# A hybrid decoder layer on one core: seven products for w_down in twelve steps of the second group, and weight loads kept in program order

## The chip, the cores and the metric

The kernel runs on one core of a Trainium2 chip. The metric is the device time of one execution in microseconds (us). Times of several runs are given as a median; a profile is one execution of its own, with its own time.

## The reference, cut to what matters

The reference is one inference step of a layer with two head groups (an mLSTM and a sliding-window attention), an output projection, and an MLP with a squared ReLU, for a prompt of 2048 tokens and a small decode batch of 32 rows. All arithmetic is in float32. The part around the change is

```python
mix = jnp.concatenate([y_m, y_a], axis=-1) @ lp['w_out']
x = x + rms_norm(mix, lp['norm_mix_post'])
u = rms_norm(x, lp['norm_ffn_pre'])
f = jnp.square(jax.nn.relu(u @ lp['w_up'])) @ lp['w_down']
x = x + rms_norm(f, lp['norm_ffn_post'])
x = x + jax.nn.sigmoid(x @ lp['w_pgate']) * (p @ lp['w_pproj'])
```

with D = 1024 model columns, 4096 hidden columns (w_up is 1024 x 4096, w_down 4096 x 1024), and 16 blocks of 128 tokens.

## The kernel before, in words

**Matmuls in three passes.** Every operand is split into a high part h (a cast on ScalarE, ACT) and a low part l (the value less h, on VectorE or on GpSimd, POOL), and `mm3` adds three matmuls, hh + hl + lh, into PSUM. A weight tile of 128 x 512 thus needs a transfer, a cast and a subtraction the first time. Weights that are used again are stored as a pair of parts in DRAM (`keep`, `store`; tensors wk), and later uses load the pair (512 KB) with no arithmetic.

**The ring of weights.** `Ring` hands out weights in the order of `plan()`. It has five raw tiles (wr, 256 KB, L296) and seven tiles for pairs (w). `take(n)` (L338) makes the next n. `row` (L348) is one tile of 128 rows and 512 columns; `multi` takes two row blocks at once; `heads` puts one together from two transfers; `product` builds the seven combinations of a w_up block of 1024 x 256 from two transfers into tiles of the pool `wide` (wb). All loads go out on SyncE's queue (SP), as `dma`; POOL's queue, `put`, carries stores and some loads. Seven pair tiles allow the loads to run ahead of TensorE by some seven tiles.

**The order of the work.** The code is written out as one program, and instructions are put into each engine's order by the language's scheduler, which may move an instruction ahead of earlier ones if its operands and its tile are free sooner. An instruction given to `here` (L205) is kept behind the instruction that was written before it on the same engine. All matmuls go through `Flow.issue`, which does that, so TensorE's order is the program's. `Flow` also keeps a clock of its own, to which each matmul adds passes x columns / 2400 us (at least 0.107), and it has sides: generators that emit side work when the clock has passed the time that they asked for with `yield`. `tick()` steps a side whose time has come; `drain(s)` empties one, and `wait` moves the clock on while other sides are stepped. So the yields decide where in the program side work is written. The weight loads are not given to `here`.

**The stages.** First six chunks of tokens (three blocks each, the last two with two) go through the input projections, with attention (`swa`) and the mLSTM (`mls`) as sides. Then three groups follow, of two chunks each: (0 to 5), (6 to 11), and (12 to 15 with the decode rows). In each group: the output projection (`mix_mm`, tensors mo) of both chunks, the residual and norm (`mix_post`), the MLP (`mlp`, L1626), and the gate (`gate_mm`, pg). The gains of norms are broadcast into one tile by `gain` (L1451, a load on SP), from a pool with one buffer: gpost (for the output projection) and gffn (for the MLP's end) take turns in it, and `gffn = gain(...)` stands at the start of `mlp` (L1628).

**The MLP.** The 4096 hidden columns go in 16 steps of 256 (FS = 2 tiles of 128). Steps 0 and 1 (FAST) run one chunk after the other, and meanwhile VectorE builds sums of the normed input for the rest. From step 2 on both chunks go together: `up_both` (L1719) computes the four hidden tiles (two chunks, two tiles of 128 hidden columns) with seven products of half size in place of eight (a Strassen-Winograd form), each with 12 matmuls of 384 columns, 84 in all (tensors up). Then `down` (L1762) multiplies, for each chunk and each half of 512 output columns, the two hidden tiles with two rows of w_down: three blocks x 2 x 3 = 18 matmuls of 512 columns (tensors dn), 72 in a step, and adds each PSUM result into the accumulator f with VectorE (L1759). In step 15 `finished` squares f for the norm and multiplies with gffn.

In the first group weights come raw and are split; in the second and third nearly all come as pairs from DRAM.

Of the kernel before, what the change touches and what calls it, by code (L numbers as in the profile page):

```python
# [9 lines left out]
F32 = mybir.dt.float32  # L10
# [8 lines left out]
P = 128  # L19
# [51 lines left out]
LODVE = 2  # L71
STEPS = FF // (FS * P)
STORE = 2
EMBW = 3.0
# [124 lines left out]
def hybrid_layer(ctx: ExitStack, tc: tile.TileContext, A, O):  # L199
    nc = tc.nc  # L200
    act, dve, pool = nc.scalar, nc.vector, nc.gpsimd
    pe = Flow(tc)
    swa, mls, tsp = pe.side(), pe.side(), pe.side()
    dma, put = nc.sync.dma_start, nc.gpsimd.dma_start
# [48 lines left out]
    def wsplit(hi, lo, src, eng=None):  # L253
        act.copy(hi, src)  # L254
        ins = (eng or weng()).tensor_tensor(lo, src, hi.bitcast(F32), ALU.subtract)  # L255
        if pinned:
            here(ins)

    class Ring:

# [23 lines left out]
        def get(self, key, n, make):  # L284

            t = self.tile(n)
            self.store()
            if key in self.kept:
                dma(t.bitcast(U32), self.kept[key])
# [9 lines left out]
        def product(self, key, i, src):  # L299


            def make(h, l):
                if i == 0:
                    self.blocks = []
                    for e in range(2):
                        t = self.wide.tile([P, KT // 2, 2 * P], F32, tag="w", name=f"{self.nm}b{self.n}{e}")
                        dma(t, src[e * 512 : (e + 1) * 512].rearrange("(k p) n -> p k n", p=P))
                        self.blocks += [t[:, :, :P], t[:, :, P:]]
# [39 lines left out]
        def row(self, key, src, n):  # L348
            def make(h, l):
                raw = self.load(n)  # L350
                dma(raw, src)
                wsplit(h, l, raw)

            return self.get(key, n, make)

        def heads(self, key, src, j, n):


            def make(h, l):
                raw = self.load(n)  # L360
                for s in range(2):
                    o = s * 256 + j * AD
                    dma(raw[s * AD : (s + 1) * AD], src[o : o + AD])
                wsplit(h, l, raw)

            return self.get(key, n, make)

        def multi(self, key, srcs, kn, n):
            three = lambda v: v.rearrange("p (k n) -> p k n", k=kn)

            def make(h, l):
                raw = self.load(kn * n)
                for off, w, s in srcs:
                    dma(three(raw)[:, :, off : off + w], s)
                wsplit(h, l, raw)
# [3 lines left out]
        def pairs(self, key, segs):  # L379


            def make(h, l):
                raw = self.load(512)
                for s, src in enumerate(segs):
                    dma(raw.rearrange("p (k s n) -> p k s n", k=2, s=2)[:, :, s], src)
                v = raw.rearrange("p (k s j c) -> p k j s c", k=2, s=2, j=2)
# [12 lines left out]
    def plan():  # L399
# [32 lines left out]
        def two(s, q):  # L432
            rows = w_up[q * P : (q + 2) * P, s * FS * P : (s + 1) * FS * P].rearrange("(k p) n -> p k n", p=P)
            return ("u", s, q), lambda key: ring.multi(key, [(0, FS * P, rows)], 2, FS * P)

        def rows_down(s):
            for half in range(2):
# [3 lines left out]
        for gi in range(len(GROUPS)):  # L441
# [12 lines left out]
            for s in range(FAST, STEPS):  # L454
                for i in range(7):
                    yield product(s, i)
                yield from rows_down(s)
            for ci in range(2):
                for half in range(2):
                    embed = 0 if half == 0 and ci == 0 else 4  # L460
                    for k in range(KT):
# [3 lines left out]
                        yield row(w_pg, k, half)  # L465

    ring.set_plan(plan())
    tpA = ctx.enter_context(tc.tile_pool(name="tpA", bufs=1))
    jp = ctx.enter_context(tc.tile_pool(name="jp", bufs=1))
# [1151 lines left out]
    wp = es2.enter_context(tc.tile_pool(name="wp", bufs=WBUF, reuse_waits="tile"))  # L1621
    sp2 = es2.enter_context(tc.tile_pool(name="sp2", bufs=2, reuse_waits="tile"))
    open_lp()
    dec = pe.side()

    def mlp(gi, chunks, sample):  # L1626
        nonlocal gffn
        gffn = gain(A["norm_ffn_post"], f"gffn{gi}")  # L1628
        G = f"{gi}"
        if sample:  # L1630
            f["t"] = es2.enter_context(tc.tile_pool(name="ft", bufs=1, reuse_waits="tile")).tile(
# [19 lines left out]
        def hidden(s, ci, ft, t, src, hid):  # L1651
# [6 lines left out]
            if sample:  # L1658

                for e, y in enumerate(hid[ci, ft]):  # L1660
# [3 lines left out]
                    else:  # L1664
                        pool.tensor_copy(y[:, W : W + HS], hid["s", ft, e])

        def temp(nm, n):
# [51 lines left out]
        def up_both(s, X, hid):  # L1719

            W = X[0][0].shape[2]
            nm = f"{G}{s}"
            turn = iter(X)

            def product(n):
                ps = psum(ps_s, f"up{nm}{n}")[:, :W]
                w, x = ring.take()[0], next(turn)
                for k in range(4):
                    mm3(ps, [t[:, k] for t in w], [t[:, k] for t in x], k == 0, k == 3)
                    pe.tick()  # L1730
                return ps

            t = [wp.tile([P, UW], F32, tag="re", name=f"re{nm}{n}")[:, :W] for n in range(4)]
# [52 lines left out]
        for ci in range(2):  # L1786
            if ci == 1:
# [4 lines left out]
                tp = es_t.enter_context(tc.tile_pool(name="tp", bufs=1, side="right", reuse_waits="tile"))  # L1792
                ring.wide = es_t.enter_context(tc.tile_pool(name="wide", bufs=WIDE, side="right", reuse_waits="tile"))
                tsp.add(sums())
# [8 lines left out]
        last_sum()  # L1803
        for s in range(FAST, STEPS):
            hid = {}
            up_both(s, X, hid)
            if s == STEPS - 1:
                es_t.close()
                open_lp()
# [195 lines left out]
```

## Time and profile before

| | us |
|---|---|
| median of 3 runs | 2610.94 (2605.71 to 2612.57) |
| the profiled execution, its time | 2623.78 |
| its span, first to last instruction | 2621.7 |
| TensorE busy in 1575.53 to 1951.77 (steps 2 to 13, second group) | 376.24 of 376.24 |
| TensorE busy in 100 to 680 (chunks 1 to 5) | 555.9 of 580 |
| TensorE busy in 780 to 1290 (first group's MLP) | 502.03 of 510 |
| TensorE busy in 2200 to 2530 (third group's MLP) | 330.00 of 330 |

Lines of the profile name engines PE (TensorE's matmuls), PEld (its weight loads), DVE (VectorE), ACT, POOL and SP; SPq is SP's queue, in which the transfers of weights wait their turn. L148 is the line of every matmul, so matmuls are told apart by their tensors' names. A row of the timeline has the start, the time, the engine, line, operation, output and inputs, the number of instructions merged, and in brackets how long the engine stood before and who released it. A row of groups has the count, the busy time, the mean of one in ns, and the idle time before. A row of waits has the time in total, how often, and the longest. Matmuls overlap, so the time of one is read from the distance between starts. PEclk is the clock that TensorE was granted, 1.00 being all of it.

### The profile page before, as it was taken

Reading aid. Unit: us, or ns where it says so; the run is one execution under the profiler, and the core shown is the slowest. Engines: PE = TensorE matmul, PEld = TensorE weight load, DVE = VectorE, ACT = ScalarE, POOL = GpSimd, SP = SyncE. Lnnn points to the kernel's source line nnn. Section 1 sums busy time; section 2 is a strip of 40 time slices with the busy share of each in tenths; the row PEclk is TensorE's granted clock in tenths of the full one; section 3 lists DMA queues with packets and bytes.
Section 4 is the critical chain, followed back from the end, with each engine's and each line's share of the span. In section 5 each row is a group of like instructions: output and inputs, shape, how many; then the busy total and the mean of one; then the engine's idle time right before and its main releaser. Section 6 shows DMA issues by size and latency. Waiting matters only on the chain.

```text
span 2621.7 us, 39337 instructions
## 1 busy us (share of the span) xinstructions
PE 2534.7 (97%) x14260; PEld 2204.3 (84%) x14260; DVE 1483.0 (57%) x3162; ACT 974.3 (37%) x2167; POOL 620.3 (24%) x988
## 2 busy tenths in 40 slices
PE   7999999998999999999999999999999999999998
PEld 7787888777778888888877788999998879999986
DVE  6666656665657655656744654444446346444553
ACT  5545444544445444444523342222223134222231
POOL 5311111112433666666523200000001011000010
PEclk9999999999999999999999999999999999999999
DMA  9756656576898666666799765555556899777787
GB/s 315 273 192 201 207 181 213 194 244 227 260 343 287 254 250 253 244 254 251 271 341 318 255 201 188 188 191 188 187 187 233 295 334 359 253 255 256 256 299 235
DMA packets 220433, 651.10 MB, mean 248 GB/s; under 512 B 25397, under 2 KB 59401, under 8 KB 220224
## 3 DMA queue, kind: packets, MB, share of 16 engines
q1 hardware_dynamic: 170032, 474.02, 53.4%
q0 software_dynamic: 50160, 174.54, 17.3%
q8 instruction: 113, 1.85, 0.3%
q14 instruction: 80, 0.66, 0.1%
q10 hardware_dynamic: 48, 0.03, 0.0%
HBM read 494.34 MB, written 155.25 MB: 248 GB/s over the span
## 4 chain that ended last, share of the span: by engine, by line
PE 77%; DVE 8%; DMA 7%; issue 3%; ACT 2%; POOL 2%; SPq 0%; ACTq 0%; DVEq 0%; POOLq 0%
PE up L148 21%; PE dn L148 21%; PE mo L148 5%; PE pg L148 5%; PE v L148 3%; DMA w<-wk 3%; PE o L148 3%; DMA wk<-w 2%; PE qk L148 2%; PE qa L148 2%; PE gv L148 2%; DVE hl L232 2%; PE aT L152 1%; PE aO L148 1%; PE pv L148 1%
## 5 line engine op out<-in xcount | busy, mean ns | idle before, releaser
L148 PE MATMUL dn<-w,hh 128*128 128x512 f32 x1792 | 564.0, 396 | 6.3 <-ACT re L1654 3.8
L1759 DVE TENSOR_TENSOR f<-f,dn 128x512 f32<-128x512 f32 x420 | 286.9, 686 | 220.5 <-PE dn L148 218.4
L148 PEld LDWEIGHTS dn<-w,hh 128*128 128x128 f32 x1792 | 334.2, 189 | 84.7 <-DVE f L1759 6.8
L148 PE MATMUL dn<-w,hl 128*128 128x512 f32 x896 | 354.5, 396 | 1.6 <-DVE hl L232 1.6
L1734 DVE TENSOR_TENSOR re<-up,re 128x384 f32<-128x384 f32 (+1 forms) x294 | 151.9, 517 | 320.2 <-PE up L148 320.2
L148 PEld LDWEIGHTS dn<-w,hl 128*128 128x128 f32 x896 | 168.8, 188 | 43.5 <-DVE hl L232 5.1
L1735 ACT COPY re<-up 128x384 f32<-128x384 f32 (+1 forms) x42 | 18.8, 448 | 392.0 <-PE up L148 392.0
L1654 ACT ACTIVATE re<-re 128x384 f32<-128x384 f32 (+1 forms) x168 | 83.0, 494 | 207.5 <-DVE re L1734 203.9
L232 DVE TENSOR_TENSOR hl<-re,hh 128x384 fp32r<-128x384 f32 (+1 forms) x192 | 137.6, 717 | 16.8 <-ACT hh L231 15.7
L282 POOL DMA_DIRECT2D wk<-w x242 | 134.1, 556 | 34.4 <-DVE w L255 25.2
L254 ACT CAST w<-wr 128x512 fp32r<-128x512 f32 (+2 forms) x152 | 88.9, 597 | 95.9 <-PE up L148 32.3
L254 ACT CAST w<-wb 128x512 fp32r<-128x512 f32 x98 | 60.6, 620 | 168.4 <-PE dn L148 114.6
L255 POOL TENSOR_TENSOR w<-wr,w 128x512 fp32r<-128x512 f32 (+2 forms) x76 | 100.2, 1319 | 80.5 <-ACT w L254 79.5
L255 POOL TENSOR_TENSOR w<-wb,w 128x512 fp32r<-128x512 f32 x70 | 92.3, 1319 | 110.3 <-ACT w L254 109.8
L1460 POOL DMA_DIRECT2D x<-x1d x16 | 8.7, 545 | 463.5 <-PE up L148 449.4
L1655 ACT ACTIVATE re<-re 128x384 f32<-128x384 f32 (+1 forms) x192 | 94.9, 494 | 5.9
L231 ACT CAST hh<-re 128x384 fp32r<-128x384 f32 (+1 forms) x192 | 92.6, 482 | 8.3
L1067 ACT ACTIVATE s<-s,swt 128x257 f32<-128x257 f32 (+1 forms) x128 | 63.3, 496 | 65.8 <-DVE swt L1064 65.8
L1061 DVE CUSTOM_DVE_ANT_0 s<-aS,cst,sink 128x256 f32<-128x256 f32 (+1 forms) x128 | 57.1, 472 | 52.0 <-PE aS L148 51.6
L148 PE MATMUL up<-t2h,w 128*128 128x384 f32 (+1 forms) x336 | 85.1, 320 | 0.0
L148 PE MATMUL up<-t0h,w 128*128 128x384 f32 (+1 forms) x336 | 85.1, 320 | 0.0
L148 PE MATMUL up<-t1h,w 128*128 128x384 f32 (+1 forms) x336 | 85.1, 320 | 0.0
(1526 smaller groups left out, 6415.7 us busy)
## 6 DMA issues: line engine op xcount, KB each, us to landing
w<-wk SPq DMA_DIRECT2D x728, 512.0 KB, 4.9
wk<-w POOLq DMA_DIRECT2D x238, 512.0 KB, 7.2
wr<-in_w_down_dram SPq DMA_DIRECT2D x64, 256.0 KB, 8.2
wb<-in_w_up_dram SPq DMA_DIRECT2D x28, 512.0 KB, 6.9
w<-wk SPq DMA_DIRECT2D x20, 528.0 KB, 3.9
x<-in_x_prompt_dram SPq DMA_DIRECT2D x16, 512.0 KB, 4.4
y<-yd SPq DMA_DIRECT2D x32, 256.0 KB, 7.0
xr<-in_x_prompt_dram POOLq DMA_DIRECT2D x16, 512.0 KB, 9.4
```

Source lines behind the costliest of these rows:

```text
L148: ins = self.pe.matmul(out, lhsT, rhs, start=start, stop=stop)
L231: act.copy(hi, src)
L232: dve.tensor_tensor(lo, src, hi.bitcast(F32), ALU.subtract)
L254: act.copy(hi, src)
L255: ins = (eng or weng()).tensor_tensor(lo, src, hi.bitcast(F32), ALU.subtract)
L282: here(put(self.kept[key], t.bitcast(U32)))
L1061: dve.tensor_tensor_reduce(s_[:, s, lo : 2 * P], pS[:, s, lo:], bias[:, j, lo:], 1.0 if s == 0 else 0.0625, sink[:, h : h + 1], ALU.add, A ...
L1067: act.activation(e_, e_, AF.Exp, bias=nm[:, s : s + 1], accum_out=sm[:, s : s + 1])
L1654: act.activation(t, src, AF.Relu)
L1655: act.square(t, t)
L1734: add = lambda out, a, b: dve.tensor_tensor(out, a, b, ALU.add)
L1759: dve.tensor_tensor(out(i), out(i), ps, ALU.add)
```

## The change

There are two parts.

**Loads in the program's order.** Every weight load of the ring goes through `wload`, which gives it to `here`. Other loads on SP (gains, tokens, y, p, Wt) are as before.

**Seven products for w_down.** In the second group, for steps 2 to 13 taken in pairs, `up_seven` computes the four hidden tiles as `up_both` does and from them four block sums (s1 = a21 + a22, s2 = s1 - a11, s3 = a11 - a21, s4 = a12 - s2; a12 is chunk 0's second hidden tile), with splits. `down_seven` then does seven products, each over three blocks, both steps and three passes (18 matmuls), in place of eight: the hidden tiles and sums with three rows of w_down (k1 and k0 for the first half of columns, k1 for the second) and four differences of them. A product's PSUM result is added by VectorE into one or two places: parts of f, or a shared sum U of three tiles, two of which lie in the buffer of gpost and gffn. After step 13 `share` adds U into three quarters of f on POOL, and only then gffn is asked for in this group.

The differences are computed once: `differences`, a side (`prep`) added before chunk 1 of the projections, loads the four blocks of each step's w_down rows into four raw tiles, subtracts on VectorE, and stores four differences (td) to DRAM, all pinned. It is drained after the last chunk. In the second group they come as raw loads with a cast on ACT and a subtraction on POOL. The pool `wide` is closed at step 2 of that group to make room, and `sp2` has one buffer for two.

```diff
+SEVEN = range(2, STEPS - 2)
+SGROUP = 1
+DIFW = 16.0, 4.0, 8.0
...
-    swa, mls, tsp = pe.side(), pe.side(), pe.side()
+    swa, mls, tsp, prep = [pe.side() for _ in range(4)]
...
+    def wload(out, src):
+
+        here(dma(out, src))
...
             if key in self.kept:
-                dma(t.bitcast(U32), self.kept[key])
+                wload(t.bitcast(U32), self.kept[key])
...
+        def diff(self, key, src):
+            def make(h, l):
+                raw = self.load(512)
+                wload(raw, src)
+                wsplit(h, l, raw, pool)
+
+            return self.get(key, 512, make)
...
+            for i, k, half in ((0, 1, 0), (0, 0, 0), (3, 0, 0), (4, 0, 0), (1, 0, 0), (0, 1, 1), (2, 0, 0)):
+                for s in steps:
+                    yield diff(s, i) if i else row(w_down, s * FS + k, half)
...
+    def differences():
+
+        sub = lambda out, a, b: here(dve.tensor_tensor(out, a, b, ALU.subtract))
+        for s in SEVEN:
+            b11, b21, b12, b22 = b = [ring.load(512) for _ in range(4)]
+            for n, t in enumerate(b):
+                k = s * FS + n % 2
+                here(put(t, w_down[k * P : (k + 1) * P, n // 2 * 512 : n // 2 * 512 + 512]))
+            yield DIFW[0]
+            for i, out, x, y in ((1, b11, b12, b11), (3, b12, b22, b12), (2, b22, b22, b11), (4, b21, b21, b22)):
+                sub(out, x, y)
+                yield DIFW[1]
+            for i, out in ((1, b11), (3, b12), (2, b22), (4, b21)):
+                here(put(td[s, i], out))
+            yield DIFW[2]
...
     for ci, blocks in enumerate(CHUNKS):
+        if ci == 1:
+            prep.add(differences())
         project(ci, blocks)
     pe.drain(swa)
+    pe.drain(prep)
...
     def mlp(gi, chunks, sample):
         nonlocal gffn
-        gffn = gain(A["norm_ffn_post"], f"gffn{gi}")
         G = f"{gi}"
+        if gi != SGROUP:
+            gffn = gain(A["norm_ffn_post"], f"gffn{gi}")
...
+            uses = (
+                ("12", out(0, 0)),
+                ("11", u, out(0, 0)),
+                ("s3", out(1, 1), out(1, 0)),
+                ("22", out(1, 0)),
+                ("s1", out(1, 1), out(0, 1)),
+                ("s4", out(0, 1)),
+                ("s2", u),
+            )
+            for n, (a, *to) in enumerate(uses):
+                w = [[t[:, :512] for t in w] for w in ring.take(2)]
+                for i in range(len(c0)):
+                    ps = psum(ps_mm, f"ds{G}{s}{n}{i}")
+                    for e in range(2):
+                        mm3(ps, [y[:, cols(i)] for y in As[e][a]], w[e], e == 0, e == 1)
+                        pe.tick()
+                    for m, o in enumerate(to):
+                        if first and n == 1 and m == 0:
+                            act.copy(o(i), ps)
+                        else:
+                            dve.tensor_tensor(o(i), o(i), ps, ALU.add)
+
+        def share(U):
+
+            for ci, half in ((0, 1), (1, 0), (1, 1)):
+                for i, b in enumerate(chunks[ci]):
+                    v = f[b][:, half * 512 : half * 512 + 512]
+                    pool.tensor_tensor(v, v, U[i], ALU.add)
...
         for s in range(FAST, STEPS):
+            if gi == SGROUP and s in SEVEN:
+                if s == SEVEN[0]:
+                    es_w.close()
...
+                    hq, wq = side("hq", 5), side("wq", 1)
+                    U = gp.tile([P, 2, 512], F32, tag="g", name=f"us{G}")
+                    U = [U[:, 0], U[:, 1], side("us", 1).tile([P, 512], F32, name=f"ut{G}")]
+                    As = []
+                As.append(up_seven(s, X, hq, wq))
+                if len(As) == 2:
+                    down_seven(s, As, U, s == SEVEN[1])
+                    As = []
+                if s == SEVEN[-1]:
+                    share(U)
+                    gffn = gain(A["norm_ffn_post"], f"gffn{gi}")
+                continue
             hid = {}
             up_both(s, X, hid)
```

More of the change, by code (lines that the diff above doesn't have):

```diff
@@ new lines, in share, with products, product @@
+        def share(U):
[3 more added lines that the diff above has]
+                    pool.tensor_tensor(v, v, U[i], ALU.add)
+        def products(s, X):
+            turn = iter(X)
+            def product(n):
+                ps = psum(ps_s, f"up{G}{s}{n}")[:, : X[0][0].shape[2]]
+                w, x = ring.take()[0], next(turn)
+                for k in range(4):
+                    mm3(ps, [t[:, k] for t in w], [t[:, k] for t in x], k == 0, k == 3)
+                    pe.tick()
+                return ps
+            return product
@@ L1722, in up_both @@
             nm = f"{G}{s}"
[L1723 to L1731, printed above, removed]
+            product = products(s, X)
             t = [wp.tile([P, UW], F32, tag="re", name=f"re{nm}{n}")[:, :W] for n in range(4)]
```

77 lines of the change are left out of this document (69 added, 8 removed).

## The prediction

> **What bounds the kernel now.** I read the page first, then the chain of work that ended last, then stages.
>
> ```profile
> span 2621.7 us, 39337 instructions
> ...
> PE 2534.7 (97%) x14260; PEld 2204.3 (84%) x14260; DVE 1483.0 (57%) x3162; ACT 974.3 (37%) x2167; POOL 620.3 (24%) x988
> ...
> PE 77%; DVE 8%; DMA 7%; issue 3%; ACT 2%; POOL 2%; SPq 0%; ACTq 0%; DVEq 0%; POOLq 0%
> ```
>
> TensorE is busy for 2534.7 of 2621.7 us, so only two things can move the time: fewer matmuls, or a change in the 87 us in which TensorE stands. The change does both. The chain shows the steps of the second group:
>
> ```profile
> 1575.53 14.74 PE up L148 x84
> 1590.27 16.80 PE dn L148 x72
> ...
> 1935.18 16.59 PE dn L148 x72
> 1951.77 14.70 PE up L148 x84
> ```
>
> Steps 2 to 13 are the twelve pieces of dn from 1590.27 to the end of the one at 1935.18; with their ups they fill 1575.53 to 1951.77, 376.24 us. The window table says how tight that is, beside two steps of the first group, which also split fresh weights:
>
> ```profile
> core 0: us, PE busy (x) PEld busy (x) DVE busy (x) ACT busy (x) POOL busy (x), PEclk, DMA share, GB/s
> 1575.53:1951.77 376.24, 376.24 (x1873) 338.60 (x1873) 170.04 (x279) 81.56 (x157) 0.00 (x0) 1.00 0.56 185
> 878.65:942.78 64.13, 63.65 (x314) 56.10 (x313) 38.43 (x54) 26.19 (x48) 40.33 (x45) 1.00 0.64 246
> ```
>
> TensorE has no gap there, the granted clock is 1.00, VectorE is at 45%, POOL does nothing. Matmuls taken out of this stage come off the end, if nothing else becomes late.
>
> **Part 1: seven products.** The 72 matmuls of one dn take 16.59 to 16.80 us, some 0.231 us each. Two steps need 144 now. Seven products, each over three blocks, two steps and three passes, are 126. Six pairs drop 6 x 18 = 108 matmuls, 108 x 0.231 = 24.9 us.
>
> What is added lies on other engines:
>
> ```profile
> L1759 DVE TENSOR_TENSOR f<-f,dn 128x512 f32<-128x512 f32 x420 | 286.9, 686 | 220.5 <-PE dn L148 218.4
> L1734 DVE TENSOR_TENSOR re<-up,re 128x384 f32<-128x384 f32 x196 | 108.8, 555 | 228.2 <-PE up L148 228.2
> L232 DVE TENSOR_TENSOR hl<-re,hh 128x384 fp32r<-128x384 f32 x128 | 109.3, 854 | 13.9 <-ACT hh L231 13.7
> L255 POOL TENSOR_TENSOR w<-wr,w 128x512 fp32r<-128x512 f32 x66 | 91.1, 1381 | 70.9 <-ACT w L254 70.0
> L254 ACT CAST w<-wr 128x512 fp32r<-128x512 f32 (+2 forms) x152 | 88.9, 597 | 95.9 <-PE up L148 32.3
> ```
>
> VectorE per pair: 30 accumulations for 24 (30 x 0.686 = 20.6 us), 16 adds of 384 columns (8.9) and 8 low parts (6.8): 36 us in 58.5 us of TensorE. Within the seven products it evacuates 20.6 us while TensorE takes 29.1; the tightest place is two products with two targets each, 12 x 0.686 = 8.2 us beside 8.3, behind three PSUM banks. ACT gains eight casts per pair, 4.8 us. POOL gets eight low parts of weights, 11.0 us, and twelve block sums or low parts of 384 columns, for which the trace has no row: between 1.04 us (1381 ns scaled by 384/512) and 1.38 us, so 12 to 17 us. Together 23 to 28 us in 58.5. All hidden on average. What is lost at the seams I bound from the first group: its two steps take 64.13 us where two of the second take 62.7, 1.4 us per pair with eleven split tiles a step against four here. I take 0.5 per pair, 3 us in all (0 to 9). Sum of part 1: -24.9 + 3 = -21.9 us.
>
> **Part 2: the differences of w_down.** Twelve times four subtractions (48 x 0.75 us, by the VectorE row of the same low part, below) and 96 transfers of 256 KB are put beside the projections of chunks 1 to 5.
>
> ```profile
> L255 DVE TENSOR_TENSOR w<-wr,w 128x512 fp32r<-128x512 f32 x66 | 49.3, 750 | 26.9 <-ACT w L254 24.5 <-PE ut31t L152 0.2
> 332.00:448.00 116.00, 113.50 (x758) 97.18 (x757) 75.64 (x239) 55.48 (x148) 14.18 (x36) 1.00 0.59 197
> 535.00:690.00 155.00, 144.71 (x995) 119.97 (x992) 91.23 (x280) 72.61 (x191) 37.92 (x73) 0.97 0.69 238
> ```
>
> VectorE is at 65% there and DMA at 59 to 69%; 36 us of VectorE and 25 MB over some 590 us raise these by about 6 and 12 points. TensorE's gaps are 2.5 us in a chunk of three blocks and 10.3 us over 535 to 690. I put 4 us on it, with the later start of the w_up blocks in the first group (0 to 14: the gaps doubled).
>
> The end of this work is another matter. Each step of the preparation asks for 16 + 4 x 4 + 8 = 40 us of the planner's clock. Summing that clock over its matmuls (passes x columns / 2400), chunks 1 to 5 last 488 us of it; twelve steps ask for 480, but each of 72 resumptions waits for the next tick, so eleven fit, and step 13 is left to the new drain. The drain runs the planner 41 us ahead, and whatever of the mLSTM's last chunk is due in those 41 us is written in front of the first w_out matmul, where now it lies between them:
>
> ```profile
> 681.35 0.66 PE L148 MATMUL mU<-vs,kw 128*64 128x130 f32 x8
> ...
> 700.72 0.66 PE L148 MATMUL mU<-vs,kw 128*64 128x130 f32 x8 [0.24 <-DVE num L1018]
> ```
>
> Six such pieces (about 4 us of TensorE), each waiting for VectorE, lose their cover: about 4 us. The preparation also holds four of the five raw tiles until its stores land, so w_out comes through one, some 6 us a tile, where two tiles last 4.2 us: another 4 us. Together 8 (2 to 18).
>
> **Part 3: loads in the program's order.** A load given to `here` is issued after whatever was written before it on SP, and SP waits in order:
>
> ```profile
> SPq L289 <- PE up L148: 331.5, 233, 11.2
> ...
> 725.22 0.38 SPq L374 DMA_DIRECT2D wr<-in_w_up_dram  x1
> 758.99 5.04 SPq L374 DMA_DIRECT2D wr<-in_w_up_dram  x3
> 773.16 0.33 SPq L1453 DMA_DIRECT2D gffn<-in_norm_ffn_post_dram  x1
> ...
> 2160.37 6.51 SPq L289 DMA_DIRECT2D w<-wk  x4
> 2169.60 0.33 SPq L1453 DMA_DIRECT2D gffn<-in_norm_ffn_post_dram  x1
> ...
> 772.46 0.68 DVE L1468 TENSOR_TENSOR f<-f,gpost 128x512 f32<-128x512 f32 x1
> ...
> 2168.88 0.69 DVE L1468 TENSOR_TENSOR f<-f,gpost 128x512 f32<-128x512 f32 x1
> ```
>
> In the code gffn (one buffer, shared with gpost) is asked for ahead of the first w_up load of each MLP. Today those loads pass it: they stand before it in SP's order. Pinned, they stand behind it, and gffn waits until VectorE has read gpost for the last time (the last two rows), after the end of mo. So the prefetch of seven weight tiles is gone at that seam. TensorE went on without a gap at these places:
>
> ```profile
> 769.25 0.35 PE L148 MATMUL up<-ut00h,w 128*128 128x384 f32 x1
> ...
> 2167.06 0.29 PE L148 MATMUL up<-ut20h,w 128*128 128x272 f32 x1
> ...
> 2176.73 0.39 PE L148 MATMUL up<-ut20h,w 128*128 128x272 f32 x1 [1.57 <-DMA w<-wk]
> ```
>
> The landing times by stage (w_down's raw tiles at 770 to 800, kept tiles at 2155 to 2200 and in steps 2 to 13), and what a long gap costs besides:
>
> ```profile
> DMA to landing us min/median/max: 3.9/6.5/8.0
> ...
> w<-wk SPq DMA_DIRECT2D x26, 512.0 KB, 6.0
> ...
> w<-wk SPq DMA_DIRECT2D x134, 512.0 KB, 4.3
> ...
> 790.00:800.00 10.00, 6.17 (x19) 4.54 (x18) 10.00 (x13) 6.37 (x14) 5.46 (x6) 0.69 0.97 361
> ...
> 795.52 1.22 PE L148 MATMUL dn<-w,hh 128*128 128x512 f32 x2 [3.83 <-ACT re L1654]
> ...
> 800.72 0.62 PE L148 MATMUL dn<-w,hh 128*128 128x512 f32 x2
> ```
>
> After 3.83 us of standing, the granted clock of the window is 0.69, and the twelve matmuls from 795.52 to 800.72 took 5.20 us where 12 x 0.231 = 2.8 are due: 2.4 us on top of the gap. The Trainium skill (TensorE: Matmul & The Clock Gate, What's actually happening) has the array at half clock after an idle window of about 3.4 us until a busy one of that length; an estimate by that page is 1.7 us a gap, which would make the sum 2 us smaller. The trace agrees in kind, and its 2.4 is used.
>
> First group: gffn at 773.16, the raw tile at 773.5, landed 6.5 later, cast 0.6, low part 0.75: 781.4, a gap of 12.1 from 769.25, with the slow clock 14.5. The gap at 795 (3.83 + 2.4) then finds VectorE and ACT ahead and goes: +8.3 (6 to 16). Third group: 2169.6 + 0.4 + 6.0 = 2176.0, 8.9 after 2167.06, with the clock 11.3, less the 1.57 gap there now: +9.7 (6 to 13).
>
> Second group: gffn moves behind the shared sums, whose tile has the same buffer. Let T be the end of the last product, whose three blocks take 1.39 us each and are summed 0.7 later. POOL's nine adds (1.38 us, by the low part's row above, the nearest) start at T - 2.1, wait for the third block's sum at T + 0.7, and have read that buffer for the last time, in the eighth, at T + 9.0. Only then gffn goes, and behind it the first w_up tile of step 14: 0.4 + 4.3 later, T + 13.7. Nothing else is left for TensorE. With the clock +16.1 (10 to 20).
>
> **Sum.** -21.9 + 4 + 8 + 8.3 + 9.7 + 16.1 = +24.2 us. The profiled execution has a span of 2621.7 and a time of 2623.78; the median of the runs is 2610.94, 12.8 below it. I expect a span near 2646 and a median of 2635.
>
> **Rivals.** (1) Faster, 2601: the three gains cost nothing, since SP is held less than I read; -21.9 + 12 = -9.9. It decides if the three gaps together stay under about 4 us. For it: the waiting of SP now is harmless for thousands of us, with tiles ahead. Against it: behind a gain no tile is ahead. The Trainium skill (DMA: Bandwidth & Descriptors, Anatomy of one DMA) says that a semaphore wait happens on the issuing sequencer before dispatch; by that rule this rival falls, and the SP rows above agree. Chance 0.12. (2) No change, 2618: half of the 34 us of gaps is covered, because VectorE frees gpost sooner when TensorE stands and POOL takes the adds whose sum is ready first: -21.9 + 12 + 17 = +7. Chance 0.14. (3) Slower by more, 2661: the preparation reaches TensorE. Step 13's loads, subtractions and stores run one after the other (loads 9.4 by the row below for POOL's queue, 3 of VectorE, 5 to store), the first raw tiles of w_out wait for them, and chunks 4 and 5 lose what DMA share they have: 30 us instead of 12 for part 2, and 8 more at the seams of the pairs: +24.2 + 18 + 8 = +50.
>
> ```profile
> xr<-in_x_prompt_dram POOLq DMA_DIRECT2D x16, 512.0 KB, 9.4
> ```
>
> For it: the gaps of 10.3 us there. Against it: 31% of DMA is free. Chance 0.14.
>
> **The numbers.** The forecast has 0.60 and a range of its own of 2619 to 2652. A measurement of this kernel can tell 0.3%, 7.8 us, from no change. Faster takes rival 1: 0.12. Within 0.3%: rival 2: 0.14. Slower: the forecast and rival 3, 0.74. The range reaches from rival 1, rounded down to 2600, to just past rival 3, 2664.
>
> **What would show it.** Right: in SP's queue each gffn directly ahead of the first w_up load of groups 1 and 3 and of step 14, TensorE idle there for 9 to 14 us waiting for a weight's transfer or its low part, and a granted clock under 1 just behind; six dn pieces of 126 matmuls and 29.1 us; POOL's nine adds ending some 9 us after the last product. Wrong: up starting directly behind mo or behind the last product; a product's 18 matmuls taking over 4.5 us; or a projection longer by over 15 us.

## The result, and the profile after

The changed kernel took 2678.03 us (median of 4 runs, 2673.33 to 2681.06) where the kernel before took 2610.86 (4 runs, 2605.71 to 2612.57): a ratio of 1.0259, with a 95% interval of 1.0239 to 1.0279. It is slower by 67 us, where the prediction had 24. The profiled execution took 2679.81 us with a span of 2678.0, 56 longer than the span before. Of all executions reported here one, of the kernel with four mends below, took 5642.95 us; it is left out, and its cause is open.

The head of the page after:

```profile
span 2678.0 us, 39855 instructions
...
PE 2527.9 (94%) x14152; PEld 2194.1 (82%) x14152; DVE 1538.8 (57%) x3255; ACT 1014.7 (38%) x2254; POOL 815.0 (30%) x1213
```

TensorE has exactly the 108 matmuls less (14260 to 14152), but is busy only 7 us less and stands for 150 us, not 87. The window table after (start and end; length; busy time and count of PE, PEld, DVE, ACT, POOL; clock, DMA share, GB/s) says where:

```profile
100.00:680.00 580.00, 554.07 (x3810) 471.05 (x3808) 389.86 (x1205) 271.42 (x725) 136.39 (x303) 0.99 0.72 253
680.00:780.00 100.00, 76.78 (x332) 59.62 (x333) 54.11 (x107) 37.54 (x83) 34.65 (x51) 0.86 0.80 273
...
1615.24:1991.54 376.30, 355.20 (x1765) 317.75 (x1763) 200.41 (x322) 123.42 (x243) 147.70 (x129) 0.99 0.60 198
```

The steps with seven products, up to the first up of step 14, take 376.30 us, as long as before (376.24), with 355.20 of TensorE in them. The w_out stretch (680 to 780) has a quarter of its time empty. TensorE's rows behind the longest gaps, and the first up of the third group, which has none:

```profile
685.69 1.53 PE L151 MATMUL mS<-qks,qks 64*128 64x128 f32 x8 [6.22 <-DVE m14f L990]
...
712.22 0.79 PE L151 MATMUL mo<-w,x6h 128*128 128x512 f32 x1 [7.53 <-ACT w L257]
...
796.45 0.69 PE L151 MATMUL up<-ut00h,w 128*128 128x384 f32 x1 [9.58 <-ACT w L257]
...
1599.53 0.72 PE L151 MATMUL dn<-w,hh 128*128 128x512 f32 x2 [4.22 <-ACT re L1703]
...
1991.54 0.69 PE L151 MATMUL up<-ut10h,w 128*128 128x384 f32 x1 [11.31 <-DMA w<-wk]
...
2210.15 0.29 PE L151 MATMUL up<-ut20h,w 128*128 128x272 f32 x1
...
2650.14 1.19 PE L151 MATMUL pg<-w,xt21h 128*128 128x512 f32 x2 [8.11 <-DMA w<-wk]
```

SP's own order at the first ups of the first group, of step 14 and of the third group, and in the last gate:

```profile
789.61 0.33 SPq L1501 DMA_DIRECT2D gffn<-in_norm_ffn_post_dram  x1
789.99 9.22 SPq L264 DMA_DIRECT2D wr<-in_w_up_dram  x7
...
1985.67 0.33 SPq L1501 DMA_DIRECT2D gffn<-in_norm_ffn_post_dram  x1
1986.11 12.49 SPq L264 DMA_DIRECT2D w<-wk  x9
...
2206.88 3.10 SPq L264 DMA_DIRECT2D w<-wk  x3
2212.68 0.33 SPq L1501 DMA_DIRECT2D gffn<-in_norm_ffn_post_dram  x1
...
2641.84 1.73 SPq L1994 DMA_DIRECT2D out_dram<-ot  x2
2645.90 0.33 SPq L1994 DMA_DIRECT2D out_dram<-ots  x1
2646.32 13.66 SPq L264 DMA_DIRECT2D w<-wk  x10
```

In the first group and ahead of step 14 the gain stands in front of the loads, as forecast. In the third group loads went in front of the gain and TensorE runs on. In the last gate the output stores of the first half (`finish` sends them through `dma` when `last` is set) stand in front of the weights of the second half and wait for the first half's last values. The prediction did not have that one.

To put a price on each stretch I follow the time at which TensorE starts a piece of work, after less before (us, from the timelines of the two profiled executions):

| start of | before | after | shift | added by the stretch that ends here |
|---|---|---|---|---|
| chunk 1 | 139.8 | 132.0 | -7.8 | chunk 0: -7.8 |
| chunk 5 | 575.5 | 576.3 | +0.8 | chunks 1 to 4: +8.6 |
| first w_out matmul | 680.6 | 695.2 | +14.7 | chunk 5 and the drain: +13.9 |
| w_out, second chunk | 726.9 | 749.0 | +22.1 | w_out, first chunk: +7.4 |
| first up, first group | 769.2 | 796.5 | +27.2 | the first gain: +5.1 |
| first gate | 1293.9 | 1318.6 | +24.8 | first MLP: -2.4 |
| w_out, second group | 1390.6 | 1422.0 | +31.3 | first gate: +6.5 |
| first up, second group | 1487.8 | 1517.1 | +29.3 | w_out, second group: -2.0 |
| step 2, second group | 1575.4 | 1615.1 | +39.7 | steps 0 and 1: +10.4 |
| step 14 | 1951.6 | 1991.5 | +39.9 | seven products and the gain behind them: +0.2 |
| first up, third group | 2167.1 | 2210.2 | +43.1 | steps 14 and 15, gate, w_out: +3.2 |
| last gate | 2535.1 | 2581.7 | +46.6 | third MLP: +3.5 |
| end of the span | 2621.7 | 2678.0 | +56.3 | last gate: +9.7 |

The two executions lie 12.8 and 1.8 us above the medians of their kernels, so the table adds up to 56.3 and not to 67. A row holds to some 3 us: in the run below in which only the last stores are moved, rows ahead of the last gate differ from these by up to 3.5 us, and by 11.4 in sum.

Within steps 2 to 13, the last product's matmuls end at 1980.2, 365.0 us after 1615.24. So twelve steps save 11.2 us in place of 21.9, and the gap of 11.31 takes that back. The chain of waits shows one seam, the same in all six pairs:

```profile
1615.24 23.19 PE up L151 x132
1640.23 5.60 DMA wr<-td
1645.84 1.57 POOL w L258 x2
1647.41 0.94 issue
1648.34 1.03 POOL s L1757
1649.96 0.60 DVE f L1796
1650.57 0.81 issue
1651.38 1.37 DVE hl13a L1727
1652.75 0.61 DVE f L1796
1653.40 22.59 PE ds L151 x96
```

A difference lands late; POOL waits to split it; the block sum s stands behind that on POOL; VectorE, which takes s3 out of the tile that POOL still reads, waits for s; and behind VectorE's wait stand the sums that free PSUM for TensorE.

### The profile page after: what moved, and what is told of

It reads as the page before. It is cut to its first block, busy times and chain, and to the rows that moved or that the text cites. A ratio compares the mean times of both kernels' runs of the same rounds, so it can differ in the third digit from the quotient of the medians.

```text
span 2678.0 us, 39855 instructions
## 1 busy us (share of the span) xinstructions
PE 2527.9 (94%) x14152; PEld 2194.1 (82%) x14152; DVE 1538.8 (57%) x3255; ACT 1014.7 (38%) x2254; POOL 815.0 (30%) x1213
## 3 DMA queue, kind: packets, MB, share of 16 engines
q0 software_dynamic: 57840, 199.71, 19.8%
## 5 line engine op out<-in xcount | busy, mean ns | idle before, releaser
L151 PE MATMUL dn<-w,hh 128*128 128x512 f32 x1216 | 383.4, 396 | 6.3 <-ACT re L1703 4.2
L151 PEld LDWEIGHTS dn<-w,hh 128*128 128x128 f32 x1216 | 226.1, 188 | 59.5 <-ACT re L1703 4.7
L1901 DVE TENSOR_TENSOR f<-f,dn 128x512 f32<-128x512 f32 x276 | 187.3, 686 | 138.9 <-PE dn L151 138.3
L151 PE MATMUL dn<-w,hl 128*128 128x512 f32 x608 | 240.1, 395 | 0.1
L258 POOL TENSOR_TENSOR w<-wr,w 128x512 fp32r<-128x512 f32 (+2 forms) x124 | 161.0, 1305 | 134.3 <-ACT w L257 110.8
L289 POOL DMA_DIRECT2D wk<-w x242 | 133.8, 555 | 17.3 <-DVE w L258 10.4
L1796 DVE TENSOR_TENSOR f<-f,ds 128x512 f32<-128x512 f32 x144 | 94.2, 683 | 30.1 <-PE ds L151 26.2
L258 DVE TENSOR_TENSOR w<-wr,w 128x512 fp32r<-128x512 f32 (+2 forms) x76 | 73.3, 970 | 53.0 <-ACT w L257 44.1
L1703 ACT ACTIVATE re<-re 128x384 f32<-128x384 f32 (+1 forms) x120 | 57.8, 482 | 112.3 <-DVE re L1876 108.9
L1738 DVE TENSOR_TENSOR re<-up,re 128x384 f32<-128x384 f32 x84 | 46.6, 555 | 83.2 <-PE up L151 83.2
L151 PE MATMUL up<-ut10h,w 128*128 128x384 f32 x288 | 80.6, 348 | 11.3 <-DMA w<-wk 11.3
L151 PE MATMUL up<-ut00h,w 128*128 128x384 f32 x288 | 80.1, 350 | 10.0 <-ACT w L257 9.6
```

Of the source, the lines that this page charges most:

```text
L151: ins = self.pe.matmul(out, lhsT, rhs, start=start, stop=stop)
L289: here(put(self.kept[key], t.bitcast(U32)))
L1703: act.activation(t, src, AF.Relu)
L1738: add = lambda out, a, b: dve.tensor_tensor(out, a, b, ALU.add)
L1796: dve.tensor_tensor(o(i), o(i), ps, ALU.add)
L1901: dve.tensor_tensor(out(i), out(i), ps, ALU.add)
```

## The experiments

Theory A: the loss has separate places, and most of them come from the loads' order: SP waits at a gain or a store with loads behind it, td loads come late, and the scheduler writes other engines' work in another order. The rest is the drain of the preparation. Theory B: the order has slack, and the seven products and their preparation cost what is lost. All ratios below are to the kernel before in the same session, whose median was 2610.15 to 2612.13. The changed kernel was timed in the first session alone, so what a mend gains on its 2678.03 us mixes sessions; the stretch in the profile in which the mend works is the surer number.

**Each part alone.** The kernel before with the ring's loads given to `wload`, and the changed kernel with

```diff
     def wload(out, src):
-        here(dma(out, src))
+        dma(out, src)
```

> The kernel before with one edit: the ring's weight loads are kept in program order (no seven products, no differences). Theory A (the order of the loads is the larger part of the loss): chunk 0 gains about 8 us; then TensorE stands about 9 us where the first group's w_up begins, about 9 us where the second group's begins (here its gain stands ahead of the loads again), not at the third group's (a pool is opened between), and about 8 us in the last gate behind the output stores; with the slow clock behind each gap 2635 to 2645 us against 2611. Theory B (the loss comes from the seven products and their preparation, the loads have slack): within 8 us of 2611.

Measured: 2651.94 us, ratio 1.0148 (1.0118 to 1.0177), 40 us slower, 7 more than theory A had at most. Its timeline has the gaps where theory A put them, and the third group has none; the one of 4.52 was not in the expectation:

```profile
769.42 0.69 PE L148 MATMUL up<-ut00h,w 128*128 128x384 f32 x1 [9.33 <-ACT w L254]
...
1500.30 0.66 PE L148 MATMUL up<-ut10h,w 128*128 128x384 f32 x1 [12.52 <-DMA w<-wk]
...
1582.45 1.22 PE L148 MATMUL dn<-w,hh 128*128 128x512 f32 x2 [4.52 <-ACT re L1658]
...
2628.02 1.19 PE L148 MATMUL pg<-w,xt21h 128*128 128x512 f32 x2 [8.11 <-DMA w<-wk]
```

> The changed kernel with the weight loads no longer kept in program order; seven products and differences stay. Theory A: the gaps of 9.6 us at 796, 11.3 at 1992 and 8.1 at 2650 go, and chunk 0 loses its 8 us again; the drain of about 17 us ahead of w_out and the pairs' 60.2 to 61.5 us stay: 2635 to 2650 us. Theory B: 2665 us or more.

Measured: 2623.26 us, ratio 1.0043 (1.0027 to 1.0058), better than theory A's numbers, which had the seams of the pairs stay. The drain is still there (first w_out matmul at 697.2), but steps 2 to 13 now take 354.20 us:

```profile
1595.90:1950.10 354.20, 353.60 (x1765) 318.53 (x1764) 201.69 (x324) 125.70 (x244) 139.82 (x122) 1.00 0.64 210
```

That is 22.0 less than the 376.24 before; part 1 of the prediction had 21.9. Seams and the gain's gap are both gone when the order alone is taken away. Theory B has fallen: the order alone costs 40 us, the other part alone 11. The remaining 16 of the 67 need both parts. By the profiles some 22 are in the seams' late td loads and the gain behind the shared sum, less one place that the change itself removes (the gain of the second group, a gap of 12.52 in the kernel with the order alone); the rest is not told apart.

**The gains.** `gffn` is asked for in step 15, after the up products, in all groups, and no longer at the two places before it:

```diff
             up_both(s, X, hid)
             if s == STEPS - 1:
+                gffn = gain(A["norm_ffn_post"], f"gffn{gi}")
```

> The changed kernel with the gain for the MLP's end asked for in step 15 behind the up products, in all three groups, so no weight load stands behind a gain that waits. Theory A: no gap over 2 us at the first up of the first group (9.6 now) nor at step 14 of the second (11.3 now); with the slow clock behind them 20 to 27 us off 2678, 2651 to 2658. Theory B (the loads would be late there anyway, since seven pair tiles are still in use and the transfers take 4 to 8 us): gaps of 5 us or more remain, less than 10 us gained.

Measured: 2650.96 us, ratio 1.0148 (1.0127 to 1.0169), 27 us less than the changed kernel. The first up of the first group starts after a gap of 0.30 us, that of step 14 after none. There eight weight loads now stand ahead of the gain in SP's order. The gain still waits: it goes at 1973.45, when POOL has read its buffer for the last time (1965.89 + 7.53), but TensorE has tiles for that time:

```profile
1955.45 14.89 SPq L264 DMA_DIRECT2D w<-wk  x8
1973.45 0.33 SPq L1501 DMA_DIRECT2D gffn<-in_norm_ffn_post_dram  x1
...
1965.89 7.53 POOL L1801 TENSOR_TENSOR f<-f,us 128x512 f32<-128x512 f32 x6 [7.37 <-DVE us L1794]
```

**The last stores.** `put(dst, o[:n])` in place of `(dma if last else put)(dst, o[:n])`.

> The changed kernel with the output stores of the last gate on POOL's queue, as those of all other gates, so that no weight load stands behind them. Theory A: the gap of 8.1 us at 2650 and the slow clock behind it go, 9 to 11 us gained, 2667 to 2669 us. Theory B (the loads would be late there in any case): the gap stays, within 3 us of 2678.

Measured: 2665.52 us, ratio 1.0218 (1.0202 to 1.0234), 12.5 us less; TensorE's gap at the last gate's second half is gone, and SP runs there through 20 weights in a row:

```profile
2603.10 34.96 SPq L264 DMA_DIRECT2D w<-wk  x20
```

But the last gate itself gains little of the 12.5. Its matmuls end 79.0 us after it starts, against 89.6 in the changed kernel; then the end of the span comes 13.3 us behind the last matmul, against 6.8, with the last stores on POOL's queue. So the gate takes 92.3 us in place of 96.4, 4.1 less; the rest of the difference lies ahead of it, where this edit changes nothing. The gap is the store's, as theory A says, but this mend gives most of it back at the end.

**The drain.** `DIFW = 12.0, 3.0, 6.0` in place of `16.0, 4.0, 8.0`.

> The changed kernel with the preparation's pauses 12, 3 and 6 in place of 16, 4 and 8 (30 us of the planner's clock a step in place of 40), so that all twelve steps end inside the projections. Theory A (the drain of step 13 costs): the first w_out matmul comes some 15 us sooner than in the changed kernel and its second stretch (w_out through one raw tile) some 5 sooner: 2655 to 2662 us. Theory B (a denser preparation takes as much from the projections through VectorE and DMA): the gain is lost in chunks 1 to 5, 2672 us or more.

Measured: 2649.51 us, ratio 1.0143 (1.0113 to 1.0173), 28.5 us less, more than theory A had. The mLSTM's pieces lie again between the w_out matmuls, as before the change:

```profile
677.76 0.62 PE L151 MATMUL spo<-w,stS 128*64 128x512 f32 x2
678.23 0.63 PE L151 MATMUL mo<-w,x6h 128*128 128x512 f32 x2
...
679.02 0.66 PE L151 MATMUL mU<-vs,kw 128*64 128x130 f32 x8
```

In the changed kernel the last projection matmul is at 677.9 too, and the first of w_out at 695.23. w_out's second chunk starts at 721.3 here, against 749.0 there; chunks 1 to 4 add 6.8 us with the denser preparation, against 8.6. From the start of chunk 1 to w_out's second chunk the kernel takes 590.2 us, the changed one 617.0 and the kernel before 587.1: 26.8 of the 28.5 us are there. The two stretches of the drain give 25.0 of them, more than the 21.3 that they had cost, because they take 3.8 us less here than in the kernel before. So theory B's objection, that a denser preparation only moves the cost, does not hold at this density.

**The seams.** Two edits, each in the changed kernel: the loads of the differences loose, and the first block sum on VectorE.

```diff
-                wload(raw, src)
+                dma(raw, src)
                 wsplit(h, l, raw, pool)
...
-            pool.tensor_tensor(s1, t[0], t[2], ALU.add)
+            dve.tensor_tensor(s1, t[0], t[2], ALU.add)
```

> The changed kernel with only the loads of the differences (td) let loose from the program's order, all other weight loads still kept in it. Theory A (the seams of the pairs are lost since a td load stands behind pair loads that wait for their tile, though raw tiles are free, and POOL then waits with the block sums queued behind): the twelve steps take 10 to 12 us less than in the changed kernel, POOL's low parts no longer wait for td, 2665 to 2669 us. Theory B (POOL's own order or its time is the seam's limit): 2675 us or more, pairs at 60 us or more.

> The changed kernel with the first block sum of each step (s1 = a21 + a22) on VectorE in place of POOL, where it stood behind low parts of weights, so that VectorE no longer waits for it with the sums out of PSUM behind. Theory A: also closes most of the seam, 5 to 11 us gained, 2667 to 2673 us. Theory B (the seam's limit is the low parts of the td weights themselves, which TensorE waits for): under 3 us gained.

Measured: with td loose 2664.00 us, ratio 1.0214 (1.0198 to 1.0230), 14 less; with s1 on VectorE 2666.93, ratio 1.0223 (1.0208 to 1.0239), 11 less. From step 2 to step 14 they take 366.0 and 371.9 us, against 376.3; the rest of what they gained lies at places that these edits do not touch, so the stretch counts more than the medians: 10.3 and 4.4 us. The groups of POOL in these stretches, the changed kernel first (low parts of weights, td among them):

```profile
L258 POOL TENSOR_TENSOR w<-wr,w 128x512 fp32r<-128x512 f32 x48 | 63.3, 1334 | 57.0 <-ACT w L257 35.0 <-DMA wr<-td 22.0
```

With td loose:

```profile
L258 POOL TENSOR_TENSOR w<-wr,w 128x512 fp32r<-128x512 f32 x48 | 64.7, 1347 | 37.4 <-ACT w L257 37.3
```

The 22.0 us of waiting for td is gone. VectorE's subtraction t1 - t0, in the changed kernel and with s1 on VectorE:

```profile
L1758 DVE TENSOR_TENSOR re<-re,re 128x384 f32<-128x384 f32 x12 | 6.7, 559 | 27.1 <-POOL s L1757 27.1
```

```profile
L1758 DVE TENSOR_TENSOR re<-re,re 128x384 f32<-128x384 f32 x12 | 6.7, 558 | 0.4
```

VectorE's 27.1 us of waiting for s is gone, but POOL still waits 17.3 us for td there. So the late transfer is the cause, and POOL's order only hands it on to TensorE. Loose loads use raw tiles that stand free: the first five td loads go out 245 to 258 us before step 2 begins, and later five of each pair's eight go out while the pair before is at work. In order they stand behind pair loads that wait for a tile, and the first of a pair's goes out some 24 us after the pair has begun.

**The second group's start.** The loads loose in steps 0 and 1 of that group alone (a flag around them in `mlp`).

> The changed kernel with the weight loads let loose from the program's order in the second group's steps 0 and 1 alone. Theory A (with loads kept in order the language's scheduler writes the last sum's casts on ACT ahead of the last squared ReLU, which has to wait for VectorE behind them; with loose loads it writes them behind): the gap of 4.2 us at 1600 and the slow clock behind it go, 9 to 11 us gained, 2667 to 2669 us. Theory B (the gap comes from the change's other parts, such as the memory given up by the pool of w_up blocks): within 3 us of 2678.

Measured: 2666.52 us, ratio 1.0212 (1.0196 to 1.0227), 11.5 less. The first up of the group starts at +28.4 (changed kernel +29.3), step 2 at +30.5 (+39.7). So 8.3 of the 11.5 us are in this stretch. ACT's rows there, in the changed kernel:

```profile
1598.26 0.83 ACT L1867 CAST ut11h<-tl 128x768 fp32r<-128x768 f32 x1 [1.43 <-DVE tl L1866]
1599.00 0.48 ACT L1703 ACTIVATE re<-up 128x384 f32<-128x384 f32 x1
```

and with the loads of these two steps loose:

```profile
1589.42 0.49 ACT L1707 ACTIVATE re<-up 128x384 f32<-128x384 f32 x1 [1.91 <-PE up L151]
...
1600.88 0.84 ACT L1871 CAST ut11h<-tl 128x768 fp32r<-128x768 f32 x1 [2.56 <-DVE tl L1870]
```

With the loads in order, a cast of the last sum (`last_sum`) stands in front of the last squared ReLU of step 1, and has to wait for VectorE; TensorE's dn waits for that ReLU (the 4.22 at 1599.53). The scheduler wrote this order; nothing in the code around it was changed.

**All together, and a better version.** The four mends in the changed kernel; then loads in order until chunk 1 begins only, with the faster preparation; then that with s1 on VectorE and pauses of 14, 3.5 and 7; last the kernel before with loads in order until chunk 1 only.

> The changed kernel with four of the edits together, weight loads otherwise kept in order: the gain asked for in step 15, the last stores on POOL's queue, the td loads loose, the preparation's pauses 12, 3 and 6. Theory A (the losses are separate places in a row and add up): 2678 less 27, 12.5, 14 and 28.5, that is 2596 us (2590 to 2606), with about 10 us left at the second group's start. Theory B (they overlap, one stall hiding another): 2615 us or more.

> The changed kernel with two edits: weight loads are kept in program order only until chunk 1 begins, and the preparation's pauses are 12, 3 and 6. Theory A (order costs at the gains, the seams of pairs, the second group's start and the last gate, and helps in chunk 0 alone; the other cost was the drain): the 2623 us of the run without pins less 22 to 27 for the drain and w_out, less 8 for chunk 0: 2588 to 2596 us, 1% faster than before. Theory B (the preparation finished sooner, or w_out's loads let loose, take it back in the first group): 2605 us or more.

> The kernel with loads kept in order until chunk 1 alone, with the first block sum on VectorE and the preparation's pauses 14, 3.5 and 7 (35 us a step, 420 in all). Theory A (the preparation at 12, 3 and 6 crowds chunks 4 and 5, some 10 us there, and spread wider it still fits): 2590 to 2594 us. Theory B (with loose loads no more is to be had from either): 2595 to 2600 us.

> The kernel before (no seven products, no differences) with its weight loads kept in program order until chunk 1 begins and loose from there. Theory A (the order helps in chunk 0 alone, by 8 us, and the rest of what the mended kernel gained, some 5 us, is what the seven products leave after their preparation): 2602 to 2606 us. Theory B (all of the mended kernel's gain comes from chunk 0): 2595 to 2599 us. Theory C (the gain in chunk 0 is given back later): 2608 us or more.

| kernel | us | ratio (95%) |
|---|---|---|
| four mends, loads else in order | 2612.49 | 1.0005 (0.9992 to 1.0019) |
| order in chunk 0 alone, pauses 12, 3, 6 | 2597.12 | 0.9959 (0.9947 to 0.9972) |
| the same, s1 on VectorE, pauses 14, 3.5, 7 | 2599.31 | 0.9951 (0.9935 to 0.9967) |
| before, order in chunk 0 alone | 2606.36 | 0.9981 (0.9971 to 0.9992) |

The four mends together gain 65 us, not the 82 of their sum, so neither theory has the number. That does not show an overlap of 16 us. Of each single mend's gain only a part lies in the stretches where it works: 26.8 us of 28.5 for the preparation (chunk 1 to w_out), 19.8 of 27 for the gains, 10.3 of 14 for the pairs, 4.1 of 12.5 for the last stores. These are 61, and the same stretches give 56.6 with all four. So theory A's list of places holds, and the losses add up but for some 4 us. The other 21 of the 82 the single runs gained at places that their edits do not touch. Of what stays, 11.1 us is the second group's start (step 2 at +13.1, the first up at +2.0), 8.5 the first gate and 5.6 the last one.

The version with order in chunk 0 alone beats the kernel before by 0.4%, where theory A had 1%; it is 1 us above theory A's range. With s1 on VectorE and the wider pauses theory B holds: the whole is the same within the intervals, though steps 2 to 13 are 2.1 us shorter. The kernel before with order in chunk 0 comes out 0.4 us above its theory A, which it fits best. Of the 0.4%, 0.2% are chunk 0's, by the last row, so the seven products are worth some 6 us net by the ratios, whose intervals just touch (9 by the medians): 22 us in steps 2 to 13, less what their preparation takes from chunks 1 to 5 and w_out. There the kernel with pauses 12, 3 and 6 goes from -8.4 at chunk 1 to -0.5 at w_out's second chunk, where the kernel of the last row goes from -6.1 to -9.6: 11.4 us.

## Why the prediction was wrong

The direction was right, the size was not: +24.2 of span forecast, +56.3 measured. The step that failed most is that part 3 priced the order of the loads at three gains and put it at nothing everywhere else. The order alone costs 40 us, and with the change it costs 10.8 us in the pairs, 8.3 at the second group's start and some 10 in the last gate. The three gains themselves were priced too high, 34.1 us for 16.9; that this hides a part of what was left out is luck. By its steps:

- **Part 1, seven products.** The -24.9 for 108 matmuls and the cover on VectorE, ACT and POOL were right: with loose loads the stretch is 22.0 us shorter. The term "I take 0.5 per pair, 3 us in all" was mis-sized for this kernel: 24.9 - 11.2 = 13.7 us, 2.3 per pair, outside its own bound of 9. It was priced from busy times and from steps with raw loads, without asking when the td loads are issued in part 3's order. With loose td loads the 3 us hold (24.9 - 22.0 = 2.9). A change of order acts in every stretch, and I costed it at the gains alone.
- **Part 2, preparation.** +4 (0 to 14) in chunks 1 to 4 measured +8.6, inside the bounds. That step 13 falls into the drain, and both of its mechanisms, were right; "Together 8 (2 to 18)" was mis-sized: 13.9 ahead of w_out and 7.4 in it, 21.3. The pieces of the mLSTM were priced by their 4 us on TensorE, where the chain that they form through VectorE counts: they fill 678.43 to 695.23, with gaps of 6.22 and shorter.
- **Part 3, gains.** First group: a gap of 9.58, at 12.1 forecast; with what the MLP gives back +2.7, at +8.3. Behind the shared sums a gap of 11.31, and 2.2 by the clock behind it: 13.5, at +16.1. The mechanism is as forecast; POOL read the shared buffer for the last time at 1985.6, 5.4 us after the last product, not 9.0, since the scheduler put the six adds of that buffer first. The slow clock is there too: 24 matmuls took 6.46 us where 24 x 0.1755 = 4.2 are due (14.74 us for 84 in the up pieces before), 2.2 us, near the 2.4 taken; the granted clock was 0.62.

```profile
1991.54:1998.00 6.46, 6.46 (x24) 6.46 (x25) 0.00 (x0) 0.48 (x1) 0.00 (x0) 0.62 1.03 414
```

- **Part 3, third group: this step failed.** "Pinned, they stand behind it" gave +9.7; the shift there is +0.7 up to the first up. Six of the group's MLP loads stand before the gain in SP's order, as many as before the change, and up starts directly behind mo, which the prediction had named as a sign of being wrong. The likely reason is in the code: `here` ties an instruction to the one written just before it on its engine, the gain itself is not held, and the third group opens the pool `ft` between gffn and the first load, so the tie seems to end on that opening and not on the gain. No run moves it, so this reason is not shown.
- **Not foreseen at all:** steps 0 and 1 of the second group, +10.4; the last gate, +9.7; the first gate, +6.5; chunk 0, -7.8. The first two come from the order: with the loads loose they are +0.2 and -0.8. For the last gate the prediction had all that it needed: loads, and then stores on SP that wait, in the code.
- **From span to time.** "I expect a span near 2646 and a median of 2635" carried over that the profiled execution before lay 12.8 us above the median. After, it lies 1.8 above. That is 11 of the 43 us missed, and no part of the mechanism.

Rival 3 (2661) was nearest. Its 30 us for part 2 measured 29.9 (8.6 + 21.3), and its 11 at the seams 13.7; but it kept the three gains at their price and had none of the places left out, so it is in part luck that its sum comes near. Rival 1's mechanism, gains that cost nothing, holds for the third group only. Of what should have been seen, the gain ahead of the loads, the gap of 9 to 14 us, the low clock, the 126 matmuls a pair, and POOL's adds ending 9.1 us after the last product (1989.3) were there at the first group and at step 14; the 29.1 us for seven products were 30.9 to 32.2, and 29.7 with loose loads.

Open: why chunk 0 is shorter with its loads in order (the gap of 2.99 us that a transpose has there before, waiting for ACT, is gone; the medians show 4 us, 2606.36 against 2610.50 in the last experiment; the profiled execution of that kernel ends 13 us before the profiled one of the kernel before, but that one lay 12.8 above its median); what of the first gate's 6.5 us is order (5.8 with the order alone, 3.1 without it, but 3.1 to 8.5 in kernels that keep it); and why the end comes 6.5 us later when the last stores go out on POOL's queue. The pools that were made smaller were not tried by themselves.

## What to carry to other kernels

An instruction kept in program order inherits every wait that is written before it on its queue: list all that the queue carries (gains, stores, other loads), not the one that caught the eye, and check what the tie is really to. A transfer that may go early only because buffers are idle is a part of the schedule; take that freedom away and engines far from the queue come late. A side task that must end by a point has to fit with room, since what is drained there pulls other sides' chains out of their cover.

## What the runs showed of the hardware

VectorE's subtractions with both operands in SBUF take longer beside POOL. In the changed kernel's steps 2 to 13, low parts of 128 x 384 on VectorE take 548 ns a piece in the first step of a pair, where POOL stands, and 913 on the mean of three in the second, where it works beside two of them (two groups of those steps):

```profile
L1727 DVE TENSOR_TENSOR hl13a<-re,hh13a 128x384 fp32r<-128x384 f32 x3 | 2.7, 913 | 1.4 <-ACT hh13a L1726 1.4
...
L1727 DVE TENSOR_TENSOR hl12a<-re,hh12a 128x384 fp32r<-128x384 f32 x3 | 1.6, 548 | 0.0
```

One took 1.37 us, beside a subtraction of 1.21 on POOL:

```profile
1650.54 0.92 DVE L1727 TENSOR_TENSOR hl13s<-re,hh13s 128x384 fp32r<-128x384 f32 x1
1651.38 1.37 DVE L1727 TENSOR_TENSOR hl13a<-re,hh13a 128x384 fp32r<-128x384 f32 x1
1652.67 0.68 DVE L1796 TENSOR_TENSOR f<-f,ds 128x512 f32<-128x512 f32 x1
...
1650.04 1.00 POOL L1761 TENSOR_TENSOR re<-s,re 128x384 f32<-128x384 f32 x1 [0.67 <-DVE re L1758]
1651.12 1.21 POOL L1762 TENSOR_TENSOR re<-re,re 128x384 f32<-128x384 f32 x1
```

Both slow ones end 0.42 us after the instruction on POOL beside them ends (at 1651.46 and 1652.75, behind 1651.04 and 1652.33).

The sums with an operand in PSUM (ds) take 0.68 us on the mean. The Trainium skill (SBUF — State Buffer, SBUF: two separate sides) says that VectorE and GpSimd share a pair of ports, held for a whole instruction by whichever starts first, where VectorE reads two inputs from SBUF; the rows agree.

Moving work to POOL is thus not free for VectorE, which the prediction's working had left out. In the changed kernel the piece of 1.37 us lies in the chain of waits shown above; with td loose TensorE has no gap over 0.3 us within the products, so pieces as long cost nothing there.
